# A hybrid decoder in one kernel: the first product of the second layer written early into a shared buffer, its small projection moved behind four plain blocks

## The chip, the cores and the metric

The kernel runs on one core of one Trainium2 chip, as one launch. The metric is device time in microseconds (us), the median of three runs. The kernel before takes 2250.92 us (2250.6 to 2252.89).

## The reference, cut to what matters

Three decoder layers work on 256 tokens of 2048 features. Layer 1 (`block1` in the kernel) is attention with a gated branch and ends in a gate on an embedding, whose result is called `x2` here. Then 16 learned "meta" tokens are put ahead of the 256, which makes 272, and layer 2 (`layer_e`) runs a state-space branch (SSD) and a convolution branch. Layer 3 (`layer_o`) is attention again. Around the layers stand norms:

```
x    = block1(x)                         # ends: x2 = tanh-gate(x1 @ w_pg) * (p @ w_ple) + x1
h    = concat(meta, rms_norm(x2, final_g))     # 16 + 256 = 272 tokens
u    = rms_norm(h, e_norm_g)             # input of layer e
z    = u @ e_w_in                        # 2048 -> many columns; blocks of 128
dt   = softplus(u @ e_w_dt + dt_bias)    # 64 step sizes for the SSD branch
...
out  = rms_norm(h3, final_norm_g)        # 256 x 2048, written to HBM
```

Matrix products are exact in fp32: either one plain fp32 product (`proj_f32`), or a weight and an input each split in two parts (`wh` + `wl`, `uh` + `ul`) and three products of those (`proj`). A plain block needs only `uf` = x2 * feg, where feg is the product of the two norms' gains; the token's scale (`r12`, in the tile `tmp`) is multiplied in behind it. A split block needs `un = uf * r12`, split into `uh` and `ul`.

## The kernel before, in words

Features lie on the 128 partitions (16 chunks of them), tokens on the free axis. Each projection runs over blocks of 128 output features, and a block is 16 plain matmuls (L156) or 48 split ones (L120, L121, L122), summed in one of three PSUM tiles called `acc`. Weights come in pieces of 512 KB through SP's DMA queue into four SBUF buffers (tag `raw`), which plain blocks (`rawf`) and split blocks (`raw`) share; two pieces make a block. For a split block ScalarE (ACT) writes `wh` (L98) and VectorE (DVE) writes `wl` (L99), which frees the buffer.

Code is written in one order, and a scheduler then decides in which order each engine's instructions stand, by estimated readiness and priority. `K.later(n)` lowers the priority of what is written under it. Once built, the order is fixed. Buffers of one tag, and of pools that follow each other in the same memory, are reused: the first writer of a reused buffer waits for the last reader of the old content.

The place that matters most is the joint between `block1` and `layer_e`. `block1` ends with a loop over 16 blocks of `w_pg` that makes `x2`, and beside it two running sums of squares: `s2` (for `sums`, L669 and L670, from which `v` at L695 and the token scale `r12` come) and `s1` (for `ss1`, three small matmuls of `tok_sum`, L210, written under `later(1000)`, from which the first norm's scale comes: `rs_...`, three `diag` tiles, a broadcast on PE at L219, `rbh`, and 16 instructions `norm_out`, L721, that overwrite x2 with its normed value for later). `layer_e` begins with `v`, a Newton iteration for the inverse root (L185 to L194) that ends in `tmp`, and with `uf` (12 chunks on ACT at L706, 4 and the meta tokens on DVE at L704 and L700). `uf` lies in a buffer of `layer_e`'s own pool, in memory that `block1`'s pools held. Blocks 0 to 3 of `e_w_in` are plain (`NAT`). `glu()` takes two blocks: `gt` (L749) reads the second, then `early` (L751, L753) the first.

Every DMA of weights stands on SP's queue. The end of the kernel is a norm: 5 DVE products (L1249) and 5 stores (L1250), also on SP.

Of the kernel before, what the change touches and what calls it, by code (L numbers as in the profile page):

```python
# [19 lines left out]
P = 128  # L20
D = 2048
NCH = D // P
# [14 lines left out]
LATER = [1000, 1500, 100]  # L37
# [211 lines left out]
def par(K, nm, i=0, n=1):  # L249
    o = PARAM[nm][0] + i  # L250
    return K.par[:, o : o + n]


def block1(K, a):
# [4 lines left out]
    with ExitStack() as ctx:  # L259
# [4 lines left out]
        def t16(tag, dt=F32, nm=None):  # L264
            return big.tile([P, 16, S], dt, tag=tag, name=nm or tag)

# [17 lines left out]
        sqs = t16("b3", nm="sqs")  # L284
# [18 lines left out]
        nc.vector.tensor_copy(r, K.rsqrt(ss[:, 0:2], 1.0 / D, EPS1))  # L303
# [5 lines left out]
        def pj(scale=None):  # L309

            i = idx[0]
            idx[0] += 1
            if i < NFIRST:
                ps = K.proj_f32(a["w_in_fm"][i], lambda c: xin[:, c, :], S, w0 if i == 0 else None)
            else:
                ps = K.proj(a["w_in_fm"][i], XH, XL, S)
            t = wk.tile([P, S], F32, tag="k1", bufs=6, name="pj")
            if scale is None:
                nc.vector.tensor_tensor(t, ps, rb, op=ALU.mult)
            else:  # L320
                nc.vector.scalar_tensor_tensor(t, ps, scale, rb, op0=ALU.mult, op1=ALU.mult)
            return t
# [9 lines left out]
        cmpA = big.tile([P, 2, 2, 16, 2, 16], F32, tag="b3", name="cmpA")  # L332
# [90 lines left out]
        kbd = big.tile([P, 2, 2, 2, 2, S], F32R, tag="b3", name="kbd")  # L423
# [171 lines left out]
        mh, ml = K.hpool.tile([P, 16, S], F32R, tag="h", name="mh"), t16("b3", F32R, "ml")  # L595
# [44 lines left out]
        feg = K.cp.tile([P, 16], F32, name="feg")  # L640
        nc.vector.tensor_tensor(feg, par(K, "final_g", 0, 16), par(K, "e_norm_g", 0, 16), op=ALU.mult)
        for m in range(16):
# [14 lines left out]
            nc.vector.tensor_tensor(x2[:, m, META:], t, pre, op=ALU.add)  # L657
            last = m == NCH - 1
# [9 lines left out]
        sums = K.ps.tile([P, 512], F32, tag="t", bufs=2, name="ss12")[:, :T2]  # L668
        nc.tensor.matmul(sums, K.ones, s2, start=True, stop=False, skip_group_check=True)  # L669
        nc.tensor.matmul(sums[:, META:], K.ones, sq, start=False, stop=True, skip_group_check=True)  # L670
        K.feg, K.sums = feg, sums
# [6 lines left out]
def layer_e(K, a):  # L678
# [3 lines left out]
    with ExitStack() as ctx:  # L682
# [10 lines left out]
        x2, feg = K.h, K.feg  # L693
# [4 lines left out]
        uf = t16("e5", "uf")  # L698
        uh, ul = K.utile("u0", "uh"), K.utile("u1", "ul")
        nc.vector.tensor_tensor(uf[:, :, 0:META], x2[:, :, 0:META], par(K, "e_norm_g", 0, 16)[:, :, None].to_broadcast([P, 16, META]),  # L700
                                op=ALU.mult)
        for c in range(NCH):
            if c % 4 == 1:
                nc.vector.tensor_scalar(uf[:, c, META:], x2[:, c, META:], feg[:, c : c + 1], None, op0=ALU.mult)  # L704
            else:
                nc.scalar.activation(uf[:, c, META:], x2[:, c, META:], AF.Copy, scale=feg[:, c : c + 1])  # L706
# [50 lines left out]
        us = [glu()]  # L757
# [100 lines left out]
        for b in range(16):  # L858
            if b:
                us.append(glu())  # L860
            if b in (0, 15):
                conv31([b])
            elif b % 2 == 0:
                conv31([b - 1, b])
            tap(TAPS[0], None)
# [21 lines left out]
        bc = big.tile([P, 2, 8, T2], F32, tag="e5", name="bc")  # L887
# [165 lines left out]
        zb = t16("e5", "zb")  # L1053
# [33 lines left out]
        bl = t16("e5", "bl", F32R)  # L1087
# [21 lines left out]
def layer_o(K, a, out):  # L1109
# [6 lines left out]
    with ExitStack() as ctx:  # L1116
# [23 lines left out]
        oh = big.tile([P, 16, S], F32R, tag="o2", name="oh")  # L1140
# [106 lines left out]
        for lo, hi in ((0, 2), (2, 4), (4, 8), (8, 12), (12, 16)):  # L1247
            v = h3[:, lo:hi, :]
            nc.vector.tensor_tensor(v, v, rb[:, None, :S].to_broadcast([P, hi - lo, S]), op=ALU.mult)  # L1249
            nc.sync.dma_start(out[:, lo:hi, :], v)  # L1250
# [157 lines left out]
```

## Time and profile before

| | us |
|---|---|
| median of three runs | 2250.92 |
| the profiled execution | 2254.26 |
| its span in the trace | 2252.4 |
| PE busy | 2211.5 (98%) |
| DVE busy | 1636.2 (73%) |
| ACT busy | 1150.6 (51%) |

The profiled execution is 0.15% above the median, and 1.86 us of it lie outside the span. PE is the matmul engine (TensorE), PEld its weight loads, SP issues DMAs. The granted clock of PE was 0.993 of 2.4 GHz over the whole execution; in a few stretches it was 0.50, which is 1.2 GHz.

### The profile page before, as it was taken

How to read it: one execution, taken by the hardware profiler on the slowest of the kernel's cores; microseconds unless marked ns; L12 is line 12 of the kernel's file. 1: busy time of each engine (PE TensorE's matmuls, PEld its weight loads, DVE VectorE, ACT ScalarE, POOL GpSimd, SP SyncE). 2: the span in 40 equal slices, each digit the busy share in tenths (PEclk: the TensorE clock that was granted, in tenths of full speed). 3: DMA queues.
4: the chain of work that ended last, by engine and by line, in shares of the span. 5: the costliest groups of instructions: out<-in, count | busy, mean ns of one | idle time of the engine just before them, and what ended most of it. 6: DMA issues, size and time to landing. Idle time of an engine off the chain costs nothing.

```text
span 2252.4 us, 43952 instructions
## 1 busy us (share of the span) xinstructions
PE 2211.5 (98%) x17686; PEld 2147.9 (95%) x17686; DVE 1636.2 (73%) x2888; ACT 1150.6 (51%) x2031; POOL 124.5 (6%) x114
## 2 busy tenths in 40 slices
PE   8999999999999999999998899999999999999997
PEld 7998799999999998999998889999999999999997
DVE  6568787555555668999999789988666666666654
ACT  4446544444444444464557789446444544454453
POOL 0000000000000230000000011003011000000011
PEclk9999999999999999999999999999999999999999
DMA  7642455555556554564544455455655445454443
GB/s 282 217 160 94 143 185 183 188 186 184 186 195 210 185 178 142 197 232 175 178 174 151 133 181 186 148 192 174 200 174 192 169 171 173 166 172 165 166 170 121
DMA packets 126412, 398.71 MB, mean 177 GB/s; under 512 B 16832, under 2 KB 33664, under 8 KB 125696
## 3 DMA queue, kind: packets, MB, share of 16 engines
q1 hardware_dynamic: 126064, 395.89, 51.6%
q8 instruction: 139, 2.28, 0.4%
q14 instruction: 65, 0.53, 0.1%
q10 hardware_dynamic: 144, 0.01, 0.0%
HBM read 391.45 MB, written 4.40 MB: 176 GB/s over the span
## 4 chain that ended last, share of the span: by engine, by line
PE 94%; DMA 2%; DVE 2%; ACT 1%; issue 0%; SPq 0%; POOL 0%; DVEq 0%; ACTq 0%; POOLq 0%
PE acc L120 29%; PE acc L122 29%; PE acc L121 29%; PE acc L156 1%; PE yps L970 1%; DMA rawf<-in_w_in_fm 1%; DMA csb<-csd 1%; PE o_ps L509 1%; ACT m L907 1%; PE pt_ps L503 1%; PE o_ps L1223 1%; PE sp L120 1%; PE sp L122 0%; PE sp L121 0%; DVE wl L99 0%; PE o_ps L1221 0%
## 5 line engine op out<-in xcount | busy, mean ns | idle before, releaser
L98 ACT ACTIVATE wh<-raw 128x1024 fp32r<-128x1024 f32 x674 | 713.5, 1059 | 942.5 <-PE acc L121 574.3
L99 DVE TENSOR_TENSOR wl<-raw,wh 128x1024 fp32r<-128x1024 f32 x674 | 829.1, 1231 | 404.3 <-ACT wh L98 399.0
L120 PE MATMUL acc<-uh,wh 128*128 128x272 f32 (+1 forms) x1488 | 437.4, 294 | 7.6 <-DVE cacc L878 6.3
L122 PE MATMUL acc<-uh,wl 128*128 128x272 f32 (+1 forms) x1488 | 433.7, 292 | 0.0
L121 PE MATMUL acc<-ul,wh 128*128 128x272 f32 (+1 forms) x1488 | 432.2, 290 | 0.0
L120 PE MATMUL acc<-xh,wh 128*128 128x256 f32 (+1 forms) x1136 | 321.8, 283 | 0.0
L121 PE MATMUL acc<-xl,wh 128*128 128x256 f32 (+1 forms) x1136 | 321.0, 283 | 0.0
L122 PE MATMUL acc<-xh,wl 128*128 128x256 f32 (+1 forms) x1136 | 319.7, 281 | 0.0
L122 PE MATMUL acc<-ouh,wl 128*128 128x256 f32 (+1 forms) x1024 | 296.6, 290 | 0.0
L121 PE MATMUL acc<-oul,wh 128*128 128x256 f32 (+1 forms) x1024 | 294.6, 288 | 0.0
L120 PE MATMUL acc<-ouh,wh 128*128 128x256 f32 (+1 forms) x1024 | 293.7, 287 | 0.0
L120 PEld LDWEIGHTS acc<-uh,wh 128*128 128x128 f32 (+1 forms) x1488 | 280.5, 189 | 12.3 <-DVE cacc L878 8.0
L122 PEld LDWEIGHTS acc<-uh,wl 128*128 128x128 f32 (+1 forms) x1488 | 279.9, 188 | 3.0 <-issue 2.3
L121 PEld LDWEIGHTS acc<-ul,wh 128*128 128x128 f32 (+1 forms) x1488 | 280.3, 188 | 2.6 <-issue 1.5
L120 PEld LDWEIGHTS acc<-xh,wh 128*128 128x128 f32 (+1 forms) x1136 | 212.4, 187 | 1.5 <-issue 0.5
L122 PEld LDWEIGHTS acc<-xh,wl 128*128 128x128 f32 (+1 forms) x1136 | 213.1, 188 | 0.4 <-issue 0.2
L121 PEld LDWEIGHTS acc<-xl,wh 128*128 128x128 f32 (+1 forms) x1136 | 212.4, 187 | 0.5 <-issue 0.2
L122 PEld LDWEIGHTS acc<-ouh,wl 128*128 128x128 f32 x1024 | 192.5, 188 | 2.6 <-issue 2.6
L120 PEld LDWEIGHTS acc<-ouh,wh 128*128 128x128 f32 x1024 | 192.9, 188 | 0.0
L121 PEld LDWEIGHTS acc<-oul,wh 128*128 128x128 f32 x1024 | 192.7, 188 | 0.0
L847 DVE SCALAR_TENSOR_TENSOR vb<-early,par,vb 128x257 f32<-128x257 f32 (+9 forms) x330 | 149.4, 498 | 1.1 <-ACT vb L831 0.7
L204 POOL TENSOR_TENSOR sq<-sq 128x272 f32<-128x272 f32 (+1 forms) x44 | 57.4, 1305 | 704.9 <-ACT sq L201 703.9
(412 smaller groups left out, 4257.4 us busy)
## 6 DMA issues: line engine op xcount, KB each, us to landing
raw<-in_e_w_in SPq DMA_DIRECT2D x184, 512.0 KB, 3.8
raw<-in_w_in_fm SPq DMA_DIRECT2D x140, 512.0 KB, 3.6
raw<-in_o_w_in SPq DMA_DIRECT2D x128, 512.0 KB, 3.6
raw<-in_e_w_out SPq DMA_DIRECT2D x64, 512.0 KB, 4.1
raw<-in_w_up SPq DMA_DIRECT2D x32, 512.0 KB, 3.7
raw<-in_w_out SPq DMA_DIRECT2D x32, 512.0 KB, 3.8
raw<-in_w_pg SPq DMA_DIRECT2D x32, 512.0 KB, 3.7
raw<-in_o_w_out SPq DMA_DIRECT2D x32, 512.0 KB, 4.5
```

The source lines that it names most:

```text
L98: nc.scalar.activation(wh, raw, AF.Copy)
L99: ins = nc.vector.tensor_tensor(wl, raw, wh.bitcast(F32), op=ALU.subtract)
L120: mm(out, lh, rh, start=start, stop=False)
L121: mm(out, lh, rl, start=False, stop=False)
L122: mm(out, ll, rh, start=False, stop=stop)
L156: self.nc.tensor.matmul(a, raws[c // 8][:, c % 8, :], x(c), start=c == 0, stop=c == 15)
L204: self.nc.gpsimd.tensor_tensor(acc, acc, sq, op=ALU.add)
L503: nc.tensor.transpose(pt_ps[:, i, kt, :], sb[:, br, i, 128 * kt : 128 * kt + 128], K.ident)
L509: nc.tensor.matmul(o_ps[64 * i : 64 * i + 64, ts], vsw[:, kt, 256 * br + 64 * g : 256 * br + 64 * g + 64], pt[:, i, kt, :], start=False, s ...
L847: ins = nc.vector.scalar_tensor_tensor(v[:, lo:hi], u[:, lo + o : hi + o], par(K, "e_dw_w", 31 * b + k), v[:, lo:hi], op0=ALU.mult, op1=AL ...
L907: nc.scalar.activation(m, csb, AF.Relu, scale=-1.0, bias=bias)
L970: prev = nc.tensor.matmul(yps[64 * hh : 64 * hh + 64, lo:hi], xt[:, i, ti, 64 * hh : 64 * hh + 64], m, start=False, stop=k >= 6, skip_grou ...
```

## The change

Five edits. (1) A pool `f` with one buffer of 16 x 272 fp32 for all layers takes the place of one large tile in each of the three layers (`b3`, `e5`, `o2`). (2) `uf` lies in it and is written in `block1`'s `w_pg` loop, chunk by chunk, all 16 on ACT (now L666; the meta tokens on DVE, L648); the matmuls of `sums` (now L679, L680) come under `later(4)`. (3) Two `glu()`, that is four plain blocks, are written ahead of `e_w_dt`'s projection in place of one. (4) In `block1`, the split of projection number NFIRST + 1 and its matmuls are written to be issued after the copy of the token scale `r`. (5) The last stores are six, with the last four chunks in two, and go to SP's and ACT's queue in turn.

```diff
-LATER = [1000, 1500, 100]
+LATER = [1000, 1500, 100, 4]
@@
+        self.fpool = ctx.enter_context(tc.tile_pool(name="f", bufs=1))
@@
+    def ftile(self, name, dt=F32, shape=(P, 16, T2)):
+
+        return self.fpool.tile(list(shape), dt, tag="f", name=name)
@@
-        sqs = t16("b3", nm="sqs")
+        sqs = K.ftile("sqs", shape=(P, 16, S))
@@
-        nc.vector.tensor_copy(r, K.rsqrt(ss[:, 0:2], 1.0 / D, EPS1))
+        r_ins = nc.vector.tensor_copy(r, K.rsqrt(ss[:, 0:2], 1.0 / D, EPS1)).ins
@@
-                ps = K.proj(a["w_in_fm"][i], XH, XL, S)
+
+                with tc.issue_after(r_ins) if i == NFIRST + 1 else nullcontext():
+                    ps = K.proj(a["w_in_fm"][i], XH, XL, S)
@@
+        uf = K.uf = K.ftile("uf")
+        nc.vector.tensor_tensor(uf[:, :, 0:META], x2[:, :, 0:META], par(K, "e_norm_g", 0, 16)[:, :, None].to_broadcast([P, 16, META]),
+                                op=ALU.mult)
         for m in range(16):
@@
             nc.vector.tensor_tensor(x2[:, m, META:], t, pre, op=ALU.add)
+            nc.scalar.activation(uf[:, m, META:], x2[:, m, META:], AF.Copy, scale=feg[:, m : m + 1])
@@
-        sums = K.ps.tile([P, 512], F32, tag="t", bufs=2, name="ss12")[:, :T2]
-        nc.tensor.matmul(sums, K.ones, s2, start=True, stop=False, skip_group_check=True)
-        nc.tensor.matmul(sums[:, META:], K.ones, sq, start=False, stop=True, skip_group_check=True)
-        K.feg, K.sums = feg, sums
+        with K.later(LATER[3]):
+            sums = K.ps.tile([P, 512], F32, tag="t", bufs=2, name="ss12")[:, :T2]
+            nc.tensor.matmul(sums, K.ones, s2, start=True, stop=False, skip_group_check=True)
+            nc.tensor.matmul(sums[:, META:], K.ones, sq, start=False, stop=True, skip_group_check=True)
+        K.sums = sums
         with K.later(LATER[0]):
             ss = K.ps.tile([P, 512], F32, tag="o", bufs=1, name="ss1")
             K.tok_sum(TN, s1, ss)
@@
-        uf = t16("e5", "uf")
+        uf = K.uf
         uh, ul = K.utile("u0", "uh"), K.utile("u1", "ul")
-        nc.vector.tensor_tensor(uf[:, :, 0:META], x2[:, :, 0:META], par(K, "e_norm_g", 0, 16)[:, :, None].to_broadcast([P, 16, META]),
-                                op=ALU.mult)
-        for c in range(NCH):
-            if c % 4 == 1:
-                nc.vector.tensor_scalar(uf[:, c, META:], x2[:, c, META:], feg[:, c : c + 1], None, op0=ALU.mult)
-            else:
-                nc.scalar.activation(uf[:, c, META:], x2[:, c, META:], AF.Copy, scale=feg[:, c : c + 1])
@@
-        us = [glu()]
+        us = [glu(), glu()]
@@
         for b in range(16):
-            if b:
+            if b > 1:
                 us.append(glu())
@@
-        for lo, hi in ((0, 2), (2, 4), (4, 8), (8, 12), (12, 16)):
+        for k, (lo, hi) in enumerate(((0, 2), (2, 4), (4, 8), (8, 12), (12, 14), (14, 16))):
             v = h3[:, lo:hi, :]
             nc.vector.tensor_tensor(v, v, rb[:, None, :S].to_broadcast([P, hi - lo, S]), op=ALU.mult)
-            nc.sync.dma_start(out[:, lo:hi, :], v)
+            (nc.scalar if k % 2 else nc.sync).dma_start(out[:, lo:hi, :], v)
```

The built order is shown at three places, all at the joint. Line numbers of the changed kernel are 3 to 10 above those of before: L156 is now L161, L210 is L215, L219 is L224, L99 is L104, L164 is L169, L695 is L705, L711 is L714, L721 is L724, L749 is L752.

PE, before, from the last split matmuls of `w_pg` to the first of `e_w_dt`. A row is one instruction, or several alike with their count behind x; `ss_9943` is the tile of `sums`, `ss_9946` that of `tok_sum`, and the rows with 64x272 are `e_w_dt`:

```order
L121 MATMUL acc<-x1l,wh 128x256
L122 MATMUL acc<-x1h,wl 128x256
L669 MATMUL ss_9943<-s_8585,ones 128x272
L670 MATMUL ss_9943<-sqw,ones 128x256
L210 MATMUL ss_9946<-ones,s_8584 128x1 x3
L156 MATMUL acc<-uf,rawf 128x272 x32
L120 MATMUL acc<-uh,wh 64x272
L121 MATMUL acc<-ul,wh 64x272
L219 MATMUL rb_10062<-diag,ones 128x128
L122 MATMUL acc<-uh,wl 64x272
```

PE at the same place in the changed kernel (`ss_9964` is `sums`, `ss_9967` is `tok_sum`):

```order
L126 MATMUL acc<-x1l,wh 128x256
L127 MATMUL acc<-x1h,wl 128x256
L679 MATMUL ss_9964<-s_8588,ones 128x272
L161 MATMUL acc<-uf,rawf 128x272 x13
L680 MATMUL ss_9964<-sqw,ones 128x256
L161 MATMUL acc<-uf,rawf 128x272 x35
L215 MATMUL ss_9967<-ones,s_8587 128x1 x3
L224 MATMUL rb_10065<-diag,ones 128x128 x3
L161 MATMUL acc<-uf,rawf 128x272 x16
L125 MATMUL acc<-uh,wh 64x272
```

The three matmuls of `tok_sum` stood ahead of all plain blocks and now stand behind 48 plain matmuls (blocks 0, 1 and 2); behind them come all three broadcasts, then block 3 and `e_w_dt`.

DVE in the changed kernel, from the last square of x2 to the first `diag` (left out are the Newton steps between `y` and `u`); before, the row of `sqw` is followed directly by `v`, and no `wl` stands between it and `un`:

```order
L669 SCALAR_TENSOR_TENSOR sqw<-x_8585,fe_8590 128x256
L104 TENSOR_TENSOR wl<-raw,wh 128x1024
L705 TENSOR_SCALAR v<-ss_9964 128x272
...
L104 TENSOR_TENSOR wl<-raw,wh 128x1024
L196 TENSOR_TENSOR u<-t,v 128x272
L196 TENSOR_TENSOR rs_u<-rs_t,rs_v 128x3
L104 TENSOR_TENSOR wl<-raw,wh 128x1024
L197 SCALAR_TENSOR_TENSOR w<-u 128x272
L197 SCALAR_TENSOR_TENSOR rs_w<-rs_u 128x3
L198 TENSOR_SCALAR w<-w 128x272
L198 TENSOR_SCALAR rs_w<-rs_w 128x3
L199 TENSOR_TENSOR tmp<-w,y_9985 128x272
```

The first of these `wl` is that of `e_w_dt`; the second and third are the first two pieces of a split block of `e_w_in`.

DVE in the changed kernel, further on, to `gt`, which reads the `acc` of block 1 (left out are pairs of `ul` and `un` alone); before, `gt` stands behind the 16 `un` too, but the 16 instructions of `norm_out` come some 100 us later:

```order
L223 TENSOR_SCALAR diag<-ident,rs_y_10079 128x128 x2
L104 TENSOR_TENSOR wl<-raw,wh 128x1024
L169 TENSOR_TENSOR ul<-un,uh 128x272
L714 TENSOR_TENSOR un<-uf,tmp 128x272
...
L223 TENSOR_SCALAR diag<-ident,rs_y_10079 128x128
...
L724 SCALAR_TENSOR_TENSOR x_8585<-x_8585,par,rbh 128x256 x6
...
L724 SCALAR_TENSOR_TENSOR x_8585<-x_8585,par,rbh 128x256 x6
...
L724 SCALAR_TENSOR_TENSOR x_8585<-x_8585,par,rbh 128x256 x4
...
L752 TENSOR_TENSOR gt<-acc,tmp 128x272
```

All of `norm_out` now stands between the third `diag` and `gt`. On SP the eight pieces of the four plain blocks come first, then `e_w_dt`, then the pieces of `e_w_in`.

## Rows read from the trace of the kernel before

**Rows 1.** The page's part 4, the chain that ended last, by engine.

```profile
PE 94%; DMA 2%; DVE 2%; ACT 1%; issue 0%; SPq 0%; POOL 0%; DVEq 0%; ACTq 0%; POOLq 0%
```

**Rows 2.** Timeline of PE at the joint: start, length, instruction, xrecords, [wait <-releaser].

```profile
845.36 0.62 PE L669 MATMUL ss<-s,ones 128*128 128x272 f32 x2
847.50 0.70 PE L670 MATMUL ss<-sqw,ones 128*128 128x256 f32 x2 [1.52 <-DVE sqw L660]
848.29 0.83 PE L210 MATMUL ss<-ones,s 128*128 128x1 f32 x6
850.09 2.13 PE L156 MATMUL acc<-uf,rawf 128*128 128x272 f32 x4 [0.97 <-ACT uf L706]
...
866.31 0.49 PE L120 MATMUL acc<-uh,wh 128*64 128x272 f32 x1
...
872.71 14.83 PE L156 MATMUL acc<-uf,rawf 128*128 128x272 f32 x64
887.17 0.49 PE L120 MATMUL acc<-uh,wh 128*128 128x272 f32 x1
```

**Rows 3.** Timeline of DVE at the joint, same columns.

```profile
849.21 0.44 DVE L695 TENSOR_SCALAR v<-ss 128x272 f32<-128x272 f32 x1 [1.77 <-PE ss L210]
849.57 0.42 DVE L700 TENSOR_TENSOR uf<-x,par 128x256 f32<-128x256 f32 x1
...
850.95 0.17 DVE L822 TENSOR_SCALAR dwb<-par 128x16 f32<-128x16 f32 x1
...
853.81 0.44 DVE L192 SCALAR_TENSOR_TENSOR w<-u 128x272 f32<-128x272 f32 x1
...
855.16 0.79 DVE L711 TENSOR_TENSOR un<-uf,tmp 128x272 f32<-128x272 f32 x2
855.88 0.48 DVE L218 TENSOR_SCALAR diag<-ident,rs_y 128x128 f32<-128x128 f32 x2
...
857.33 0.43 DVE L711 TENSOR_TENSOR un<-uf,tmp 128x272 f32<-128x272 f32 x1
857.68 0.43 DVE L164 TENSOR_TENSOR ul<-un,uh 128x272 fp32r<-128x272 f32 x1
...
862.43 1.23 DVE L99 TENSOR_TENSOR wl<-raw,wh 128x1024 fp32r<-128x1024 f32 x1 [1.15 <-ACT wh L98]
```

**Rows 4.** Timelines of SP's queue and of ACT at the joint, one piece of weights.

```profile
858.00 0.33 SPq L95 DMA_DIRECT2D raw<-in_e_w_dt  x1
861.34 1.06 ACT L98 ACTIVATE wh<-raw 128x1024 fp32r<-128x1024 f32 x1 [1.01 <-DMA raw<-in_e_w_dt]
```

**Rows 5.** Groups by line, DVE, 955 to 980 us: xcount, busy, mean ns.

```profile
L721 DVE SCALAR_TENSOR_TENSOR x<-x,par,rbh 128x256 f32<-128x256 f32 x16 | 6.7, 481 | 0.0
```

**Rows 6.** Windows: stretch, its length, busy of PE, PEld, DVE, ACT, POOL, clock, DMA, GB/s.

```profile
38.00:41.00 3.00, 2.77 (x7) 2.19 (x8) 3.00 (x7) 0.00 (x0) 0.00 (x0) 0.50 0.82 295
850.00:855.00 5.00, 4.91 (x14) 3.90 (x15) 5.00 (x24) 4.19 (x12) 0.00 (x0) 0.66 0.05 9
1190.00:1220.00 30.00, 23.36 (x176) 20.62 (x175) 29.61 (x68) 20.95 (x54) 1.69 (x2) 0.94 0.39 126
1265.00:1275.00 10.00, 3.67 (x22) 3.05 (x21) 7.06 (x11) 7.56 (x20) 0.00 (x0) 0.75 0.71 223
2247.00:2249.00 2.00, 0.00 (x0) 0.00 (x0) 0.69 (x1) 0.00 (x0) 0.00 (x0) 0.50 1.04 348
```

**Rows 7.** Waits of PE, 30 to 45 us, then 1190 to 1285 us: total, times, longest.

```profile
PE acc L120 <- DVE pj L319: 2.5, 1, 2.5
...
PE acc L120 <- DVE cacc L878: 6.3, 3, 3.2
```

**Rows 8.** DMA issues at the end, 2243 to 2253 us: xcount, KB each, us to landing.

```profile
out<-h SPq DMA_DIRECT2D x3, 512.0 KB, 3.2
out<-h SPq DMA_DIRECT2D x2, 256.0 KB, 2.3
```

More of the change, by code (lines that the diff above doesn't have):

```diff
@@ L262, in block1 @@
         wk = ctx.enter_context(tc.tile_pool(name="b1w", bufs=2))
-        def t16(tag, dt=F32, nm=None):
-            return big.tile([P, 16, S], dt, tag=tag, name=nm or tag)
         def t8(tag, dt=F32, nm=None):
@@ L331, in block1 @@
         pe = {nm: const_in("pe" + nm, "pe_" + nm) for nm in ("k", "v")}
-        cmpA = big.tile([P, 2, 2, 16, 2, 16], F32, tag="b3", name="cmpA")
+        cmpA = K.ftile("cmpA", shape=(P, 2, 2, 16, 2, 16))
         nc.gpsimd.memset(cmpA[:, :, 1, :, :, 15], 0.0)
@@ L422, in block1 @@
         nc.sync.dma_start(dmat, a["c_dist"])
-        kbd = big.tile([P, 2, 2, 2, 2, S], F32R, tag="b3", name="kbd")
+        kbd = K.ftile("kbd", F32R, (P, 2, 2, 2, 2, S))
         nc.gpsimd.memset(kbd.bitcast(F32), 0.0)
@@ L592, in block1 @@
                 zs.append(gate(g + 2))
-        mh, ml = K.hpool.tile([P, 16, S], F32R, tag="h", name="mh"), t16("b3", F32R, "ml")
+        mh, ml = K.hpool.tile([P, 16, S], F32R, tag="h", name="mh"), K.ftile("ml", F32R, (P, 16, S))
         for m in range(16):
@@ L639, in block1 @@
         nc.vector.tensor_scalar(s2[:, 0:META], s2[:, 0:META], EPS2 * (1.0 - EPS1) * D / P, None, op0=ALU.add)
-        feg = K.cp.tile([P, 16], F32, name="feg")
+        feg = wk.tile([P, 16], F32, tag="feg", bufs=1, name="feg")
         nc.vector.tensor_tensor(feg, par(K, "final_g", 0, 16), par(K, "e_norm_g", 0, 16), op=ALU.mult)
+        uf = K.uf = K.ftile("uf")
+        nc.vector.tensor_tensor(uf[:, :, 0:META], x2[:, :, 0:META], par(K, "e_norm_g", 0, 16)[:, :, None].to_broadcast([P, 16, META]),
+                                op=ALU.mult)
         for m in range(16):
@@ L690, in k1 @@
             return wk.tile([P, T2], F32, tag="k1", bufs=NK1, name=nm)[:, :n]
-        x2, feg = K.h, K.feg
+        x2 = K.h
         v = k1("v")
@@ L885, in conv5 @@
             return nc.vector.scalar_tensor_tensor(dst, t, 1.0, acc, op0=ALU.add, op1=ALU.mult)
-        bc = big.tile([P, 2, 8, T2], F32, tag="e5", name="bc")
+        bc = K.ftile("bc", shape=(P, 2, 8, T2))
         for k in range(2):
@@ L1052, in layer_e @@
         K.defer(ln_task())
-        zb = t16("e5", "zb")
+        zb = K.ftile("zb")
         K.hook = lambda ins: tap(TAPS[4], ins)
@@ L1086, in layer_e @@
         bh = big.tile([P, 16, T2], F32R, tag="e6", name="bh")
-        bl = t16("e5", "bl", F32R)
+        bl = K.ftile("bl", F32R)
         for c in range(NCH):
@@ L1138, in layer_o @@
         QH, QL = (lambda c: qv(uh, c)), (lambda c: qv(ul, c))
-        oh = big.tile([P, 16, S], F32R, tag="o2", name="oh")
+        oh = K.ftile("oh", F32R, (P, 16, S))
         ol = big.tile([P, 16, S], F32R, tag="o3", name="ol")
```

## The prediction

> **What bounds the kernel now.** I read the chain that ended last first: PE holds 94% of it [rows 1], so time is lost or won where PE waits or runs at the lower clock, and nowhere else. Then I listed PE's waits and the stretches with a clock under 1. Four places remain: the start (2.5 us behind `pj`, and three us at clock 0.50 [rows 6, 7]), the joint of `block1` and `layer_e`, the SSD stage (PE busy 23.36 of 30 us and 3.67 of 10, with 6.3 us of its waits on DVE's `cacc` [rows 6, 7]), and the closing norm. At the joint PE waits 1.52 us for `sqw` and 0.97 for `uf` [rows 2], and from 850 to 855 it runs at 0.66 [rows 6], which costs (1 - 0.66) x 4.91 = 1.7 us. That is all that an earlier `uf` can give back there: 4.2 us. DVE's own row says what held both `uf` and `v`: `v` waited 1.77 us for L210, the `tok_sum` matmuls, not for `sums` [rows 3]. `layer_e`'s tiles lie where `block1`'s lay, and `s1`, which L210 reads, is among these.
>
> **The joint, step by step.** Before, `uf` needed that memory too, so plain blocks could not start ahead of L210, and the scheduler had to put L210 first. In the shared buffer `uf` needs it no longer; 48 plain matmuls are ready, and L210, at the lowest priority, sinks behind them, as the built order shows. `v` still needs the memory. So I follow the built order with durations of before. A plain matmul takes 0.463 us: the group of 14.83 us is two blocks, 32 matmuls (each leaves two records) [rows 2].
>
> 1. PE runs without a wait at first: from 845.98 (845.36 + 0.62), 13 plain (6.0), L680 (0.70), 35 plain (16.2), `tok_sum` (0.83) [rows 2]: 869.7.
> 2. `v` stands on DVE behind the `wl` of `e_w_dt`. Its buffer is the one that block 2's first half frees, that is after the 40th plain matmul, at 845.98 + 6.0 + 0.70 + 27 x 0.463 = 865.2. From issue to the end of `wl` such a piece takes 862.43 + 1.23 - 858.00 = 5.66 us [rows 3, 4]. So `wl` ends at 870.9, and `v`, freed by `tok_sum` at 869.7, starts at 870.9: in before it was 849.21.
> 3. From `v` to the first `un` before: 855.16 - 849.21 = 5.95 us, of which 850.95 - 849.57 = 1.38 were `uf` [rows 3] and are gone. Two more `wl` now stand inside. The second waits longest: its buffer is freed by `e_w_dt`'s `wl` at 870.9, plus 5.66 makes 876.5. From `w` to `un` it was 1.35 us [rows 3], so `un` starts at 877.9. Two `un` and the first `diag` take 0.72 + 0.24 [rows 3]: PE's first broadcast at 878.9. **PE is idle 869.7 to 878.9: 9.2 us.**
> 4. A fourth `wl` follows; the first `e_w_in` piece is issued behind block 2 at 868.9 and frees its buffer at 874.6, so this piece is done at 880.3. Two pairs of `ul` and `un` at 0.35 an instruction (857.33 to 857.68 [rows 3]) and the third `diag`: 882.0. **PE is idle 2.6 us more.**
> 5. PE's next instruction is block 3. There are three `acc` tiles; block 3 gets that of block 1, which `gt` frees, and `gt` stands behind 16 `norm_out` at 6.7 / 16 = 0.42 us [rows 5] and 24 `un` and `ul` at 0.35, together 15.1 us: `gt` ends at about 897.5. **PE is idle 15.3 us**, until 897.6.
> 6. Block 3 takes 7.4 us, `e_w_dt` 6.0 (872.71 - 866.31 less the broadcast of 0.4 inside it [rows 2]): 911.0. Before, the same work ended at 887.17 [rows 2], its 1.7 us of low clock included. Difference +23.8.
> 7. Clock: behind the start's idle 2.5 us PE ran at 0.50 for three us [rows 6], so I put 2.0 us of loss behind the two long gaps (1.5 to 3). The Trainium skill, "TensorE: Matmul & The Clock Gate", section "HAM oscillation — how this bites in real kernels", speaks against this change in the same way: PE that idles for a DMA or another engine starts its next run at the slow clock, and pays at each such gap. By it the loss here would be that of two gaps, about twice the 1.5 us that the start's three us at half clock cost, an estimate of 3 against my 2; the start's row agrees with it for one gap.
>
> Joint: **+25.8 us**. The low bound is +22.7, with no loss of clock and `norm_out` at the 0.35 of its neighbours (16 x 0.07 = 1.1 less); the high one +30, with 3 us of clock, `norm_out` at its mean of 0.48 [rows 5] (+1.0) and two pieces each 1 us longer on their way.
>
> **The other edits.** `uf` on ACT in the loop: 16 x 0.4 us on an engine that is half idle and two steps off PE; nothing. The shared buffer in the attention stages only renames a buffer; nothing. *Token scale:* `pj` now stands behind one `wl` fewer (1.2 us earlier), but two `wl` are put behind the scale's chain, so their buffers and the next DMAs are up to 1.7 us later; -0.5, from -3.9 (the wait of 2.5 and 0.5 x 2.77 = 1.4 of clock vanish [rows 6, 7]) to +1.5. *SSD stage:* DVE is full there (29.61 of 30 us [rows 6]) and is 6.7 us of `norm_out` lighter ahead of it [rows 5]; but PE is full and DVE not bound for 200 us between, so little of that is carried: -1.5, from -6.3 (all of the `cacc` wait [rows 7]) to +3 for the order shuffled by the scheduler. *Last stores:* a last piece of 256 KB lands in 2.3 us, one of 512 KB in 3.2 [rows 8]: -0.9 if nothing else limits. But the DMA engines are busy throughout 2247 to 2249 (share 1.04 [rows 6]), so a second queue only interleaves what is moving; -0.5, from 0 to -0.9. The Trainium skill, "Trainium Kernel Development and Optimization", section "Key Constraints", states that SP's and ACT's queues run on the same 16 DMA engines and that issuing from several saves only issue time. By it the gain would be the low end, near 0; the full share in the row agrees.
>
> **Sum:** 25.8 - 0.5 - 1.5 - 0.5 = +23.3. The profiled execution (2254.26) would become 2277.6; it lies 3.3 above the median, so for the median of 2250.92 I say 2274.2 us.
>
> **The rivals.**
>
> *A, the stall is paid back (not slower).* While PE waits, DVE gets ahead, `norm_out` included; if the SSD stage then ran without PE waits, it would return 30 - 23.36 and 10 - 3.67, that is 13.0 us of idle PE and, at the clocks of 0.94 and 0.75 [rows 6], up to 4 more; start and tail give up to 4.8: 21.8 in all. With the joint at +25.8 that ends at 2254.9, with +22.7 at 2251.8. It decides only if nearly all of it comes back (18.2 with the low joint, 21.3 with mine). Against it: only 6.3 of these waits are DVE's `cacc`; and PE is full, so DVE's lead is bounded by four weight buffers. 3 in 100.
>
> *B, the cover works (faster).* If `v` did not need L215, or if the fourth block were not held by `gt`, PE would have 29.7 us of plain blocks to cover the 6 us up to `un` and 32 `un` and `ul` at 0.35; the 4.2 us of the joint and the 1 to 3 of start, tail and SSD would be gained: 2244. Against it: the wait of `v` on L210 [rows 3] and, apart from it, `e_w_dt`'s `wl` ahead of `v`, which alone keeps `v` at 870.9. 3 in 100.
>
> *C, half a stall (slower by less).* If the second and fourth `wl` found their DMAs landed, steps 3 and 4 shrink by some 4 us, and with -6.3 in the SSD stage, -3.9 at the start and -0.5 at the end the sum is +11.1: 2262. 15 in 100 for 2262 to 2268.
>
> *D, a longer stall.* Behind 911 us only few pieces of split weights are ready, and four `hres` stores stand ahead of ten weight loads on SP; each block needs two pieces in 5.9 us. If the stream is late once or twice, +4 to +8: 2278 to 2282. 15 in 100.
>
> The forecast itself, 2268 to 2278, gets 60; the rest lies in A, B or farther out.
>
> **How the numbers follow.** The likeliest sum is 2274.2. C and D give the ends: 2262 to 2282 holds a little over 8 in 10. Less than 0.2% (4.5 us) is about what a measurement of this kernel can't tell from no change. Faster has B and part of A, 0.04; the same has the rest of A, 0.03; slower 0.93.
>
> **What would show it.** In the changed kernel's trace PE has three gaps between 868 and 900 us, in front of L224 (twice) and of L161, the last put down to `gt` L752 or to what stands before it; `v` starts near 871, behind `wl`; block 3 starts near 897. Step 2 is wrong if `v` starts before 866, step 5 if block 3 starts before `norm_out` ends. `e_w_dt` that ends by 890 would make the whole prediction wrong. `cacc` waits under 3 us in the SSD stage would show A's mechanism at work, and a wait of PE for `pj` under 1 us the gain at the start.

## The result, and the profile after

| | before | after |
|---|---|---|
| median, us | 2251.9 (2250.6 to 2256.62, 4 runs) | 2281.8 (2280.34 to 2284.12, 4 runs) |
| ratio of after to before | | 1.0125, 95% interval 1.0113 to 1.0138 |
| profiled execution, us | 2254.26 | 2280.67 |
| span, us | 2252.4 | 2278.7 |
| PE busy, us | 2211.5 | 2218.8 |

The change makes the kernel 29.9 us slower where 23.3 was forecast; 2281.8 lies just inside the range of 2262 to 2282. Between the two profiled executions it is 26.4 us. The other 3.5 come from how these two lie to their medians: that of before is 2.4 above its own, that of after 1.1 below. One execution of tok_now, further down, ran at a granted clock of 0.75 and took 2687.0 us, where the others of it took 2259 to 2266; it is left out.

To see where the 26.3 us of span arose, I compared the start of the same PE instruction in both traces. Behind the first and the second split block these are small sums on the token axis: `yss` ends the SSD stage, `lns` and `lnv` enclose the layer norm, `fss` stands at the end.

| PE instruction | before | after | later by | since the row above |
|---|---|---|---|---|
| first matmul of `sums` (L669, now L679) | 845.36 | 843.16 | -2.2 | -2.2, the start |
| first split block behind `e_w_dt` and the plain ones | 887.17 | 911.50 | +24.3 | +26.5, the joint |
| `yss` | 1425.9 | 1450.8 | +24.9 | +0.6, the SSD stage |
| `lns` | 1515.2 | 1540.1 | +24.9 | 0 |
| `lnv` | 1547.9 | 1574.3 | +26.4 | +1.5, the layer norm |
| `fss` | 2237.78 | 2264.21 | +26.4 | 0 |
| end of the span | 2252.4 | 2278.7 | +26.3 | -0.1, the closing norm |

From the first row to `yss` PE has 4319 matmul records in either trace, and 711 more to `lns`, so the rows compare equal work.

All of the loss stands at the joint. This is PE's timeline there in the changed kernel, which answers to [rows 2] (start, length, instruction, records, wait):

```profile
843.16 0.62 PE L679 MATMUL ss<-s,ones 128*128 128x272 f32 x2
843.62 6.12 PE L161 MATMUL acc<-uf,rawf 128*128 128x272 f32 x26
849.58 0.59 PE L680 MATMUL ss<-sqw,ones 128*128 128x256 f32 x2
...
866.05 0.72 PE L215 MATMUL ss<-ones,s 128*128 128x1 f32 x6
877.40 1.22 PE L224 MATMUL rb<-diag,ones 128*128 128x128 f32 x4 [10.63 <-DVE diag L223]
880.34 0.80 PE L224 MATMUL rb<-diag,ones 128*128 128x128 f32 x2 [1.72 <-DVE diag L223]
895.48 10.18 PE L161 MATMUL acc<-uf,rawf 128*128 128x272 f32 x32 [14.34 <-DVE gt L752]
```

The wait of before for `sqw` is gone and so is that for `uf`: PE runs from 843 to 866.8 without a gap. Then come three gaps, in the three places forecast: 10.63, 1.72 and 14.34 us, together 26.7. Block 3, in the last row, takes 10.18 us for 16 matmuls where a plain block of before took 7.4. And this is DVE over the same stretch, which answers to [rows 3]:

```profile
866.96 1.23 DVE L104 TENSOR_TENSOR wl<-raw,wh 128x1024 fp32r<-128x1024 f32 x1 [21.71 <-ACT wh L103]
868.10 0.43 DVE L705 TENSOR_SCALAR v<-ss 128x272 f32<-128x272 f32 x1
...
873.93 1.22 DVE L104 TENSOR_TENSOR wl<-raw,wh 128x1024 fp32r<-128x1024 f32 x1 [1.32 <-ACT wh L103]
...
876.36 0.79 DVE L714 TENSOR_TENSOR un<-uf,tmp 128x272 f32<-128x272 f32 x2
...
880.00 0.28 DVE L223 TENSOR_SCALAR diag<-ident,rs_y 128x128 f32<-128x128 f32 x1
...
882.31 2.46 DVE L724 SCALAR_TENSOR_TENSOR x<-x,par,rbh 128x256 f32<-128x256 f32 x6
...
894.99 0.44 DVE L752 TENSOR_TENSOR gt<-acc,tmp 128x272 f32<-128x272 f32 x1
```

The first row is the one to look at: DVE did nothing for 21.71 us. Its queue was headed by the `wl` of `e_w_dt`, whose weights could be fetched only when PE's block 2 had freed a buffer, and `v` stood behind it. `tok_sum`, whose end `v` needed as well, ended at 866.8 and this `wl` at 868.2, so either alone would have held `v` nearly as long. PE's gaps are the other side of the same delay.

The clock, in two windows around the return of PE's work (columns as in [rows 6]):

```profile
895.00:900.00 5.00, 4.52 (x10) 3.48 (x11) 4.14 (x11) 1.46 (x3) 0.00 (x0) 0.50 0.00 0
900.00:905.00 5.00, 5.00 (x21) 4.06 (x21) 4.17 (x9) 0.00 (x0) 0.00 (x0) 0.93 0.29 105
```

From 895 to 900 PE works at 0.50, that is at 1.2 GHz, and at 0.93 in the next five us: the 10.18 us of block 3 hold 2.6 us of low clock (the same block at full clock takes 7.58 us in own_s1, below).

In the SSD stage PE still waits, a little less than before (waits of PE, 1200 to 1320 us):

```profile
PE yps L970 <- DVE yb L975: 4.4, 1, 4.4
PE acc L125 <- DVE cacc L881: 3.3, 1, 3.3
PE yps L973 <- DVE m L912: 1.8, 1, 1.8
PE cbps L927 <- ACT cb L925: 1.0, 1, 1.0
```

That is 10.5 us, against 13.0 in before (6.3 for `cacc`, 3.6 for `m`, 3.1 for `four`). The stores at the end answer to [rows 8]:

```profile
out<-h SPq DMA_DIRECT2D x2, 256.0 KB, 3.0
out<-h ACTq DMA_DIRECT2D x2, 256.0 KB, 2.9
```

A piece of 256 KB takes 2.9 to 3.0 us to land where it took 2.3 before. From the first `fss` matmul to the end of the span it is 14.6 us before (2252.4 - 2237.78) and 14.5 after.

### The profile page after: what moved, and what is told of

It reads as the page before. It is cut to its first block, busy times and chain, and to the rows that moved or that the text cites. A ratio compares the mean times of both kernels' runs of the same rounds, so it can differ in the third digit from the quotient of the medians.

```text
span 2278.7 us, 43932 instructions
## 1 busy us (share of the span) xinstructions
PE 2218.8 (97%) x17686; PEld 2153.4 (95%) x17686; DVE 1636.8 (72%) x2885; ACT 1151.7 (51%) x2035; POOL 116.4 (5%) x114
## 4 chain that ended last, share of the span: by engine, by line
PE 95%; DVE 2%; DMA 2%; ACT 1%; issue 0%; SPq 0%; DVEq 0%; ACTq 0%
PE acc L125 29%; PE acc L127 29%; PE acc L126 29%; PE acc L161 1%; PE yps L973 1%; DMA rawf<-in_w_in_fm 1%; PE o_ps L513 1%; PE pt_ps L507 1%; PE o_ps L1226 1%; DVE wl L104 1%; PE sp L125 0%; PE sp L127 0%; PE sp L126 0%; PE o_ps L1224 0%; ACT wh L103 0%; DMA raw<-in_w_in_tm 0%
## 5 line engine op out<-in xcount | busy, mean ns | idle before, releaser
L104 DVE TENSOR_TENSOR wl<-raw,wh 128x1024 fp32r<-128x1024 f32 x674 | 828.5, 1230 | 424.9 <-ACT wh L103 418.2
```

What stands on the lines that cost most here:

```text
L104: ins = nc.vector.tensor_tensor(wl, raw, wh.bitcast(F32), op=ALU.subtract)
```

## The experiments

The theory: `v` waits for `tok_sum` because its memory was `s1`'s, and `tok_sum`, which no plain block needs any longer, sinks behind 48 matmuls. The first rival: the four plain blocks ahead of `e_w_dt` cause the stall, whatever `v` does. A second question came up in the first runs: whether time won at the joint lasts until the end. Each ratio is against runs of the kernel before on the same chip (medians 2253.7 to 2254.6 there).

**own_s1**, the changed kernel with `s1` in memory that nobody reuses:

```diff
-        s1, s2 = [wk.tile([P, T2], F32, tag="s12", name="s12") for _ in range(2)]
+        s1 = K.cp.tile([P, T2], F32, name="s1")
+        s2 = wk.tile([P, T2], F32, tag="s12", bufs=1, name="s12")
```

> The changed kernel with s1 in memory of its own that no later pool reuses; tok_sum keeps its low priority and still stands behind 48 plain matmuls. Theory (v waits for tok_sum only because its memory was s1's): v starts right behind the sums, near 851 us, un near 856, gt before PE reaches block 3; the three gaps of 26.7 us and the slow clock behind them are gone, median 2245 to 2249. Rival (the four plain blocks ahead of e_w_dt, and block 3 held by gt, make the stall whatever v does): at least 10 us of gap in front of block 3 stay, 2262 or more.

Measured: 2254.46 (2249.85 to 2257.69, 11 runs), ratio 1.0000 (0.9992 to 1.0009). PE at the joint:

```profile
848.68 0.59 PE L681 MATMUL ss<-sqw,ones 128*128 128x256 f32 x2
849.12 16.20 PE L161 MATMUL acc<-uf,rawf 128*128 128x272 f32 x70
865.16 0.72 PE L215 MATMUL ss<-ones,s 128*128 128x1 f32 x6
865.75 7.58 PE L161 MATMUL acc<-uf,rawf 128*128 128x272 f32 x32
```

`tok_sum` still stands behind 48 plain matmuls, and nothing waits for it: no gap is left, block 3 takes 7.58 us, and DVE's `v` starts at 849.39. So the stall comes from `v`'s wait for reused memory; the first rival is out. The order on DVE changed with it: the `wl` of `e_w_dt` now stands behind all 16 `un` and starts at 865.98. The scheduler had put it ahead of `v`, so this run takes both holds away at once; one_glu, below, tells them apart.

The time expected was 2245 to 2249, and it is not reached. The first split block starts at 879.1, 8.0 us ahead of before, and 3.1 of these were there at the first matmul of `sums` (842.27). At `lns` 4.6 are left (1510.6), because PE idles 18.5 us on the way there and 15.0 in before. At `lnv` 2.6 are left (1545.3), and as much at the end of the span. The median doesn't show even these: the profiled execution, 2251.55, lies 2.9 below it. The waits that grew are in the SSD stage (waits of PE, 1180 to 1310 us):

```profile
PE yps L974 <- DVE m L913: 8.7, 2, 5.1
PE acc L125 <- DVE cacc L882: 8.5, 2, 6.3
PE xtp L998 <- ACT four L904: 1.4, 1, 1.4
```

18.6 us, against 13.0.

**tok_now** and **tok_now_again**, the changed kernel with `tok_sum` at the priority of the sums (one kernel, run twice; the trace read here is that of the second):

```diff
-        with K.later(LATER[0]):
+        with K.later(LATER[3]):
             ss = K.ps.tile([P, 512], F32, tag="o", bufs=1, name="ss1")
             K.tok_sum(TN, s1, ss)
```

> The changed kernel with tok_sum at the priority of the sums, so that its three matmuls stand two plain matmuls behind them; s1 stays where it was. Theory: as with s1 in its own memory, 2245 to 2249, since only the place of tok_sum mattered. Rival (four plain blocks): 2262 or more, with the gap in front of block 3.

> The same kernel as tok_now, for a profile at full clock; that run gave 2259 to 2266 where 2245 to 2249 was expected. If the stall is gone at the joint (e_w_dt ends near 880, no wait of PE over 1 us there) and the loss lies where DVE bounds the SSD stage (waits for cacc and for m, yps together 20 us or more against 13 before), the theory of the joint stands and the gain is paid back later. If PE still waits over 5 us at the joint, the theory is wrong.

Measured: 2262.73 and 2261.81 (2256.56 to 2266.6 in the second), ratio 1.0036 (1.0024 to 1.0048, 1.0024 to 1.0047). The stall is gone here too; in the second run's profile PE waits 1.81 us for a `diag` and 0.57 for `gt`, and the last matmul of `e_w_dt` starts at 882.5. So where `tok_sum` stands is the other half of the same cause. But both runs miss the 2245 to 2249, by 13 us, and the SSD stage doesn't account for it: PE waits 13.4 us there, as in before and not the 20 or more expected, and `yss` is at 1423.7, 2.2 us ahead of before, and `lnv` at 1551.1, 3.2 us behind. From `lns` to `lnv` it is 38.0 us here and 32.7 in before, with a wait that before doesn't have (waits of PE, 1510 to 1560 us):

```profile
PE acc L127 <- DVE wl L104: 2.7, 1, 2.7
```

Nothing of that stage was edited, but its built order is another. This is the layer norm of before on DVE and on GpSimd (POOL):

```profile
1518.22 4.67 DVE L164 TENSOR_TENSOR al<-yb,ah 128x272 fp32r<-128x272 f32 x13
1528.77 17.87 POOL L204 TENSOR_TENSOR sq<-sq 128x272 f32<-128x272 f32 x14 [0.56 <-ACT sq L201]
```

and here:

```profile
1520.38 7.23 POOL L209 TENSOR_TENSOR sq<-sq 128x272 f32<-128x272 f32 x8 [9.04 <-ACT sq L206]
1522.47 5.44 DVE L169 TENSOR_TENSOR al<-yb,ah 128x272 fp32r<-128x272 f32 x6
```

DVE's `vb` subtractions stand among its `al` here, GpSimd's running sums of squares, `sq`, begin 7.3 us behind `lns` where they began 12.2 behind it, and the six `al` that run beside them take 0.91 us each where thirteen took 0.36. In the six builds whose `sq` begin 7 to 8 us behind `lns` (own_s1 is one), `lns` to `lnv` takes 34.7 to 38.0 us, and 32.1 to 34.2 in the others, with own_s1_sums (35.2) as the exception. This is read from the traces; no run changes it alone. The remaining spread, 2256.6 to 2266.6, goes with the granted clock of the execution (0.993 at the low end, 0.990 at the high one).

**one_glu**, the changed kernel with two plain blocks ahead of `e_w_dt` again:

```diff
-        us = [glu(), glu()]
+        us = [glu()]
@@
-            if b > 1:
+            if b:
                 us.append(glu())
```

> The changed kernel with e_w_dt behind two plain blocks again; tok_sum sinks behind 32 plain matmuls instead of 48. Theory: the stall stays in smaller form. tok_sum ends near 859, un starts near 864, and e_w_dt is fed by 32 un and ul with norm_out among them until about 882; blocks 2 and 3 follow, and the first split block starts near 897 in place of 911: 2266 to 2271. Rival (the four plain blocks are the cause): the stall is gone, 2246 to 2250.

Measured: 2264.23 (2261.48 to 2267.84), ratio 1.0046 (1.0034 to 1.0058). The stall stays with two blocks, and is smaller by what `tok_sum` comes earlier; the first split block starts at 896.48, where 897 was worked out, and the time is 2 us under the 2266 to 2271 expected. Here `wl` and `tok_sum` can be told apart (DVE's timeline):

```profile
852.15 1.23 DVE L104 TENSOR_TENSOR wl<-raw,wh 128x1024 fp32r<-128x1024 f32 x1 [7.63 <-ACT wh L103]
858.81 0.44 DVE L705 TENSOR_SCALAR v<-ss 128x272 f32<-128x272 f32 x1 [5.43 <-PE ss L215]
```

`wl` is done at 853.4, and `v` waits on for L215 by itself, 5.43 us.

**before_two_glu**, the kernel before with the opposite edit:

```diff
-        us = [glu()]
+        us = [glu(), glu()]
@@
-            if b:
+            if b > 1:
                 us.append(glu())
```

> The kernel before with four plain blocks ahead of e_w_dt, nothing else. Theory: tok_sum stands ahead of all plain matmuls there, so v starts near 849 as before; no new wait, time within 0.2% of before (2249 to 2255). Rival (the four plain blocks are the cause): block 3 waits for gt, slower by 10 us or more.

Measured: 2250.2 (2248.91 to 2254.04, 11 runs), ratio 0.9988 (0.9979 to 0.9997). Four plain blocks do no harm when `tok_sum` stands ahead of them, and may be worth 2 to 3 us.

**norm_late**, the changed kernel with `norm_out` behind the second `gt`; `g_ins` holds the `gt` instructions:

```diff
             for m in range(16):
-                nc.vector.scalar_tensor_tensor(x2[:, m, META:], x2[:, m, META:], par(K, "final_g", m), rb[:, META:],
-                                               op0=ALU.mult, op1=ALU.mult)
+                with tc.issue_after(g_ins[1]):
+                    nc.vector.scalar_tensor_tensor(x2[:, m, META:], x2[:, m, META:], par(K, "final_g", m), rb[:, META:],
+                                                   op0=ALU.mult, op1=ALU.mult)
@@
-        K.run(norm_out(), LATER[0])
@@
         us = [glu(), glu()]
+        K.run(norm_out(), LATER[0])
```

> The changed kernel with its 16 norm_out instructions put behind gt of the second pair of plain blocks; all else as it was, tok_sum late. Theory (they stand in front of the gt that block 3 waits for): PE's gap in front of block 3 shrinks from 14.3 us by 16 x 0.41 = 6.6 to about 7.7, time 6 to 7 us under the changed kernel, 2274 to 2277. Rival (gt waits for something else, or the 6.6 us are paid later): 2279 or more.

Measured: 2281.82 (2278.83 to 2285.99), ratio 1.0123 (1.0109 to 1.0137). PE, block 3:

```profile
889.64 9.88 PE L161 MATMUL acc<-uf,rawf 128*128 128x272 f32 x32 [8.01 <-DVE gt L752]
```

The gap in front of block 3 is 8.01 us, 6.3 less than 14.34, so step 5 of the prediction priced `norm_out` rightly, at 6.7. The total didn't move. `e_w_dt` is 6.2 us earlier than in the changed kernel (its last matmul at 905.21 against 911.37), and at `lns` 0.5 us of this is left (1539.6 against 1540.1): PE idles 16.2 us from the first split block to there in place of 11.1. (`yss`, at 1453.7, can't be compared here: 4358 matmul records stand ahead of it in place of 4319.) Most of the idle time is waits in the SSD stage, 14.4 us in place of 10.5:

```profile
PE yps L974 <- DVE m L913: 6.9, 1, 6.9
PE acc L125 <- DVE cacc L882: 5.9, 2, 3.5
PE xtp L998 <- ACT four L904: 1.6, 1, 1.6
```

**before_r**, the kernel before with edit 4 of the change alone:

```diff
-        nc.vector.tensor_copy(r, K.rsqrt(ss[:, 0:2], 1.0 / D, EPS1))
+        r_ins = nc.vector.tensor_copy(r, K.rsqrt(ss[:, 0:2], 1.0 / D, EPS1)).ins
@@
-                ps = K.proj(a["w_in_fm"][i], XH, XL, S)
+                with tc.issue_after(r_ins) if i == NFIRST + 1 else nullcontext():
+                    ps = K.proj(a["w_in_fm"][i], XH, XL, S)
```

> The kernel before with the token scale ahead of the later splits, nothing else. PE is 2 us earlier at the joint in the changed kernel. If time won ahead of the SSD stage is kept, 2 us faster, ratio 0.999; if the DVE-bound SSD stage takes it back, ratio 1.000 and its PE waits grow by 2 us.

Measured: 2254.24 (2252.34 to 2255.8), ratio 0.9999 (0.9990 to 1.0007). PE's wait for `pj` is 1.3 us in place of 2.5, and L210 starts at 845.4 in place of 848.3. The gain is there at 845 us and not at the end, but the SSD stage doesn't take it: PE idles 12.1 us from the first split block to `yss`, 14.4 in before, and this kernel is ahead by 4.2 us at `yss` and by 3.8 at `lns`. At `lnv` it is ahead by 0.8. This is one of the six builds with early `sq`: `lns` to `lnv` takes 35.7 us in place of 32.7.

**own_s1_sums**, as own_s1, with an order that puts the second matmul of the sums (`K.sum_ins`) behind 4 plain ones:

```diff
+            with self.tc.issue_after(behind[0]) if behind is not None and c == behind[1] else nullcontext():
                 self.nc.tensor.matmul(a, raws[c // 8][:, c % 8, :], x(c), start=c == 0, stop=c == 15)
@@
-                return K.proj_f32(a["e_w_in"][i], lambda c: uf[:, c, :], T2), True
+                return K.proj_f32(a["e_w_in"][i], lambda c: uf[:, c, :], T2, behind=(K.sum_ins, 0 if i else 4)), True
```

> As own_s1, and the sums are put behind 4 plain matmuls in place of 13, so that v starts near 845 instead of 849. If DVE's lead at the joint lasts until the SSD stage, PE's waits there shrink from 18.6 us by up to 4 and the time is 2248 to 2252; if it is lost on the way, as own_s1, 2252 to 2256.

Measured: 2252.81 (2249.55 to 2255.62), ratio 0.9995 (0.9986 to 1.0003). The interval holds own_s1's 1.0000: inconclusive, and no more than 1 to 2 us. PE's waits from 1180 to 1320 us are 13.7 in place of 18.6, the 4 to 5 us less that the theory wanted, and the time didn't follow.

**own_s1_pool**, **before_two_glu_pool**, **after_pool**: three kernels with `norm_out` off DVE:

```diff
-                nc.vector.scalar_tensor_tensor(x2[:, m, META:], x2[:, m, META:], par(K, "final_g", m), rb[:, META:],
-                                               op0=ALU.mult, op1=ALU.mult)
+                nc.gpsimd.tensor_tensor(x2[:, m, META:], x2[:, m, META:], rb[:, META:], op=ALU.mult)
+                nc.scalar.activation(x2[:, m, META:], x2[:, m, META:], AF.Copy, scale=par(K, "final_g", m))
```

> As own_s1, with norm_out taken off DVE: a product on GpSimd and a scaling on ACT in place of each of the 16 DVE instructions. Theory (DVE's work between the joint and the SSD stage sets when that stage runs, so PE's lead is taken back there): DVE is 6.7 us lighter ahead of it, PE's waits for cacc and m shrink from 17 us by 4 to 7, time 2247 to 2251. Rival (these waits are set inside the stage by its own chain): the waits stay, time as own_s1, 2252 to 2256.

> As before_two_glu, with norm_out on GpSimd and ACT. Theory: 2244 to 2248, below both kernels, by the same 4 to 6 us. Rival: 2249 to 2252, as before_two_glu.

> The changed kernel with norm_out on GpSimd and ACT. PE's gap in front of block 3 shrinks as in norm_late, from 14.3 to about 8, but here DVE doesn't get the 6.7 us back later. Theory (what lasts is DVE's delay): 2273 to 2277, where norm_late kept 2282. Rival (something behind the joint other than DVE's work took norm_late's 6 us back): 2279 or more.

Measured: 2248.46 (2247.41 to 2249.99), ratio 0.9972 (0.9961 to 0.9983); 2263.31 (2258.76 to 2267.9), 1.0039 (1.0027 to 1.0051); 2283.97 (2282.92 to 2284.51), 1.0129 (1.0116 to 1.0142). One of three went as expected. before_two_glu_pool is 13 us above before_two_glu, which neither theory nor rival has; its profiled execution loses 6.5 us of it between the first split block and `lns`, and why is not shown. And the trace of after_pool says that the experiment doesn't test what it was meant to: GpSimd's products don't relieve DVE, they slow it. GpSimd's rows of after_pool:

```profile
881.60 15.35 POOL L724 TENSOR_TENSOR x<-x,rbh 128x256 f32<-128x256 f32 x16 [35.49 <-DMA raw<-in_e_w_in]
```

and DVE's:

```profile
882.75 0.43 DVE L169 TENSOR_TENSOR ul<-un,uh 128x272 fp32r<-128x272 f32 x1
...
886.59 0.96 DVE L169 TENSOR_TENSOR ul<-un,uh 128x272 fp32r<-128x272 f32 x1
...
897.17 0.43 DVE L752 TENSOR_TENSOR gt<-acc,tmp 128x272 f32<-128x272 f32 x1
```

`ul` takes 0.43 us and, from 885.7 until GpSimd ends, 0.96. The gap in front of block 3 grew to 16.78 us instead of shrinking to 8. So own_s1_pool is the fastest version, 0.28% below before, and its cause is not the one expected: DVE is busy for 532.5 us from 843 to 1422 there, and for 531.0 in own_s1. PE's waits in the SSD stage are 10.7 us in place of 18.6. That came with another built order; which part of it did it I have not shown, and 2248.46 against 2254.46 is more than the two profiled executions differ (2249.35 and 2251.55).

**own_s1_busy**, as own_s1, with idle work for DVE (nobody reads it; `g_ins` as in norm_late):

```diff
         us = [glu(), glu()]
+        for _ in range(32):
+            with tc.issue_after(g_ins[1]):
+                nc.vector.tensor_tensor(k1("un"), r12, r12, op=ALU.mult)
```

> As own_s1, with 32 more DVE products (r12 times itself, into a spare tile; nobody reads them) behind the second gt, where PE has no wait on DVE: about 32 x 0.35 = 11 us of DVE time and none of PE's. Theory (from the joint to the end of the SSD stage DVE's time counts: its busy time there is the same in all runs, 531 to 535 us, and the stretch is that plus DVE's idle): the yss matmuls, at 1422 in own_s1, come 8 to 12 us later, time 2261 to 2267. Rival (PE sets the stretch, and DVE's idle time of some 48 us takes the 11 us in): yss by 1426, time 2253 to 2258.

Measured: 2256.7 (2255.58 to 2260.16), ratio 1.0012 (1.0003 to 1.0021), which is 2 us over own_s1, and `yss` at 1425.9, 3.9 us later, `lns` at 1515.5, 4.9 later. 1.2 us of either were there at the first split block (880.33 against 879.13), ahead of the added work. That is the rival's number, not the theory's: of some 11 us of DVE work about a third reached `lns`, and a fifth the median.

## Why the prediction was right, point by point

**The number** was right with luck. 2281.8 is 7.6 us above the likeliest 2274.2, outside the forecast's own 2268 to 2278, and in the band that the prediction gave to rival D, a late stream of weights behind 911 us. That did not happen: PE has no wait between 905 and 1200 us. Of the 7.6 us, 3.1 are in the sum (2280.67 in place of 2277.6). The other 4.5 come from the median, which was put 3.3 below the profiled execution and lies 1.1 above it. The chances don't add up either: the range was given a little over 8 in 10, and its three parts sum to 90 in 100.

**What the change does at the joint** was right, and is shown. Taking `v` off the reused memory alone (own_s1) ends the stall, moving `tok_sum` alone (tok_now) ends it, and undoing the four plain blocks doesn't (one_glu). In the first two the `wl` ahead of `v` went too; that the wait for `tok_sum` holds `v` by itself is shown by the 5.43 us of one_glu. No run moved `uf` alone. That its old memory kept `tok_sum` early is read from the trace of before, where ACT's `uf` and DVE's `v` each wait 1.8 us for L210. Rival B, in which the plain blocks cover everything, is what own_s1 does at the joint, though its 2244 is not what follows.

**The sizes, step by step**, with 2.2 us off the prediction's times for the earlier start. Step 1: `tok_sum` ends at 866.8, forecast 867.5. Step 2: `v` at 868.1, forecast 868.7. Step 3: the first broadcast at 877.4, forecast 876.7; the second of the two `wl` inside was done at 875.15 where 874.3 was worked out, and `tok_sum` 0.7 earlier, and so the first gap is 10.63 in place of 9.2. Step 4: 1.72 us, forecast 2.6; from the first broadcast to the third it is 2.94 us against 3.1, and the first two took 1.22 of it, at a clock of 0.50. Step 5: 14.34 us, forecast 15.3; block 3 starts at 895.48, forecast 895.4. Steps 6 and 7: the joint costs 26.5 us against 25.8, with 2.6 us of low clock, forecast 2.0. The Trainium skill's rule on the clock gate ("TensorE: Matmul & The Clock Gate", section "HAM oscillation — how this bites in real kernels"), from which the prediction had worked out an estimate of 3 for two gaps, came a little nearer, but not by its count: the clock was 0.50 behind the first gap too, where DVE set the pace, and all 2.6 us were lost behind the last.

**The terms around the joint** are what was mis-sized, by 2.3 us together; the joint itself was by 0.7. *Token scale*: -2.2, forecast -0.5; the wait for `pj` fell from 2.5 to 1.8 us, and PE's clock from 35 to 45 us is 1.00 where it was 0.83, which is 0.17 x 7.52 = 1.3 us. I had priced the clock only as a bound. The sign named, a wait for `pj` under 1 us, did not come; the gain did. *SSD stage*: +0.6, forecast -1.5. `norm_out` is gone from the stretch ahead of it and PE's waits in it are 2.5 us shorter, but not the time. Summed over windows of 1 us from the first split block to `yss`, PE idles 10.5 us in place of 14.4 and loses 7.6 us to the low clock in place of 4.8; the last 1.7 us are not accounted for. *Layer norm*: +1.5, not forecast. PE's waits there are the same as before to 0.01 us (0.58, 0.22 and 0.56), but the clock from 1535 to 1555 is 0.87 and then 0.96, where before it stayed at 1.00. *Last stores*: -0.1, forecast -0.5. The pieces of 256 KB landed later, in 2.9 to 3.0 us in place of 2.3, while the DMA share was 1.04 from 2274 to 2276 us; the row with a full DMA share [rows 6] had said so. This agrees with the Trainium skill, "Trainium Kernel Development and Optimization", section "Key Constraints", by which the queues share the DMA engines.

**Rival A**, that the SSD stage pays the stall back, did not happen (`cacc` still costs 3.3 us, where under 3 was its sign); why is only partly settled. DVE's busy time from the joint to `yss` is nearly the same whatever the kernel; here it is in windows of before, of the changed kernel and of norm_late:

```profile
845.00:1426.00 581.00, 564.04 (x4323) 540.12 (x4322) 532.24 (x1043) 354.61 (x739) 31.16 (x28) 0.99 0.52 175
```

```profile
843.00:1451.00 608.00, 570.85 (x4322) 545.08 (x4320) 533.03 (x1038) 350.51 (x728) 28.72 (x28) 0.96 0.50 167
```

```profile
843.00:1454.00 611.00, 575.90 (x4364) 550.56 (x4362) 534.59 (x1040) 351.83 (x730) 33.61 (x29) 0.96 0.52 167
```

The third busy time is DVE's: 532, 533 and 535 us. What the changed kernel adds is 26 us of idle DVE (75 against 49), about the 21.71 us behind `wl` and the waits that follow. norm_late removed a gap of PE but none of DVE's idle time (76 us), and was no faster. That would fit a stretch that is set by DVE as much as by PE; then the sum of PE's gaps came out right because DVE had lost as much. This is argued and not shown, and own_s1_busy speaks against it: two thirds of an added 11 us of DVE work vanished before `lns`. How much of a delay on either engine survives to the end of the SSD stage stays open. What became of own_s1's lead of 8 us is told above, but not why PE waits more in its SSD stage.

## What to carry to other kernels

When a buffer is moved out of a pool, look for the waits that it had by accident: here, as the trace of before has it, the memory of `uf` was what kept three low-priority matmuls ahead of the plain blocks, and once it was gone they sank until something that still needed that memory starved. Read the built order on every engine for such sinking, and ask of each instruction that heads an in-order queue what it is waiting for; a DVE row with 21.7 us of idle time in front of it says more than any busy share. Time won ahead of a stage in which several engines wait for each other is not won until that stage's own waits have been compared, and every rebuild under a scheduler shuffles stages that were not touched: from `lns` to `lnv` these kernels took 32.1 to 38.0 us.

## What the runs showed of the hardware that was not expected

While GpSimd multiplied two SBUF tiles (15.35 us for 16), DVE's products and subtractions of two SBUF tiles took 0.96 us in place of 0.43, and `gt`, which reads one operand from PSUM, took 0.43 directly behind. The Trainium skill, "SBUF — State Buffer", section "SBUF: two separate sides", states that DVE and GpSimd share one pair of ports, and that of a DVE operation with two SBUF inputs and one of GpSimd that reads SBUF, the one that starts first holds the pair for its whole length while the other waits. The trace agrees: GpSimd's first product took 2.52 us, from 881.6, while DVE ran on at 0.43, and ended when DVE had paused; from 885.7 on DVE's operations start every 0.88 us, about one product of GpSimd (median 0.92), so each got its turn behind one of them. The layer norm of tok_now and of five other builds, which nobody edited, reads the same way: `al` also subtracts two SBUF tiles and `sq` adds two (0.91 us in place of 0.36, above). Whether an operand in PSUM escapes it can't be told from `gt`, which ran when GpSimd was done, but can from the layer norm of before. There DVE's `vb` reads one operand from SBUF and one from PSUM (`lnm`), and beside GpSimd's `sq`, which run from 1528.8 to 1546.6, it takes 0.37 us:

```profile
1531.40 1.47 DVE L1036 TENSOR_TENSOR vb<-vb,lnm 128x272 f32<-128x272 f32 x4
```

The clock fell without any wait of PE. In the changed kernel PE is busy throughout here, and the clock is 0.50 from 1054.3 to 1057.7 (columns as in [rows 6]):

```profile
1053.00:1058.00 5.00, 5.00 (x27) 4.67 (x28) 2.49 (x5) 3.94 (x11) 0.00 (x0) 0.66 0.05 17
```

Just before, from 1047.1 to 1053.9, 20 small matmuls (`dtp`, 64x64 and 64x16) stand one by one and in pairs between the split ones; in before they stand together, 0.9 us in all, and the clock stays at 1.00. The same fall stands behind `dtp` in before_r and norm_late, and not in tok_now, whose `dtp` are spread as widely. What decides it is not shown.

After equal waits of PE in the layer norm the clock was 1.00 in one build and 0.87 in another, a difference of 1.5 us. And in the same build, tok_now, executions between 2256.6 and 2266.6 us go with clocks between 0.993 and 0.990; here, differences under 5 us between builds can't be read from one execution.
